# Three quarters of a 1024 x 4096 x 1024 float32 product by seven products of block sums in place of eight

## The chip, the core and the metric

One core of a Trainium2 chip runs the kernel. The metric is the device time of one execution in microseconds; for each kernel several executions are timed and the median is told. One further execution was recorded by the hardware profiler, and all rows below come from it. The engines are TensorE (PE; its weight loads are PEld), VectorE (DVE), ScalarE (ACT), GpSimd (POOL) and SyncE (SP), which issues most DMAs. POOL issues DMAs too. Each engine runs its own instructions in a fixed order, and a wait holds up everything behind it on that engine.

## The reference

One layer of a diffusion backbone on x of [1024, 1024], all in float32. The first sub-layer mixes tokens; the second, which the change is about, is an MLP with a squared ReLU:

```
def squared_relu_mlp(h, w1, w2):
    return jnp.square(jax.nn.relu(h @ w1)) @ w2
...
    h2 = modulate(x_lat, norm_pre_ffn[l], sh2, sc2)
    x_lat = x_lat + gt2 * rmsnorm(squared_relu_mlp(h2, w_ff1[l], w_ff2[l]), norm_post_ffn[l])
```

Here w1 is [1024, 4096] and w2 is [4096, 1024].

## The kernel before

Every large product is made of three matmuls: both factors are cut into a high and a low part of the type fp32r, and `mm3` (L196) sums high x high, high x low and low x high in PSUM. The cut is `split` (L165): ACT casts to the high part (L166), DVE subtracts it from the source for the low part (L167). `product` (L898) is one bank of PSUM, 128 x 512, with 4 steps of k, so 12 matmuls.

The program has three stages on PE after the attention: the output projection and the rows of x1 (`rows`, L946, with two calls of `rstd_of` for each tile of 128 rows), the first feed-forward product (loop over j, L1106), and the second (loop over blkn, L1163).

The first feed-forward product already works with seven products of block sums for each j of 0 to 15. A j is 256 of the 4096 hidden columns. Its four results c11, c12, c21 and c22 (two blocks of 128 hidden rows by two of 512 tokens) lie in one tile `hp`, of which there are two; ACT takes ReLU and square in place (L1152, L1153), and POOL writes the tile to `hid_d[j]` in HBM (L1154). The first two results of j = 0 to 3 were made earlier (`EARLY`). b_1 (in the buffer big0), b_2 (in big1), t1, t2 and t4 are the right-hand factors.

The second product is plain: eight blocks of 512 hidden rows; in each, two loads of hidden rows (`hr`, 1 MB each) are split into `hd` (big0 and big1 in turn), two loads of w2 (`wfraw`) are split into three pairs of buffers that take turns, and 8 token tiles x 2 column halves take 12 matmuls each, so 16 x 12 = 192 matmuls a block and 1,536 in all. ACT copies the results of block 0 to `y2t` (L1193), DVE adds those of the others (L1195). In the last block ACT sums squares (L1198), POOL multiplies by g2 (L1199), and DVE takes the reciprocal root (`rsqrt`, L206, for pairs of tiles and for the tiles 6 and 7 alone) and adds x1 (L1207); SP writes the output.

A scheduler writes the order of instructions on each engine down when the program is built, from its own estimate of times. The order is fixed from then on.

## Time and profile before

| | |
|---|---|
| median of 3 timed executions | 1721.79 us (1720.53 to 1725.85) |
| profiled execution | 1719.08 us |
| its span, first to last instruction | 1717.3 us |
| PE busy | 1650.3 us, 8,691 matmuls |
| DVE, ACT, POOL busy | 893.8, 612.0, 328.6 us |
| mean granted clock of PE | 0.988 of full speed |

The profiled execution lasted 1.8 us longer than its span, and was 2.7 us shorter than the median. Matmuls overlap, so that the busy time of one (0.39 us) is more than the distance between two starts.

### The profile page before, as it was taken

Reading aid. Unit: us, or ns where it says so; the run is one execution under the profiler, and the core shown is the slowest. Engines: PE = TensorE matmul, PEld = TensorE weight load, DVE = VectorE, ACT = ScalarE, POOL = GpSimd, SP = SyncE. Lnnn points to the kernel's source line nnn. Section 1 sums busy time; section 2 is a strip of 40 time slices with the busy share of each in tenths; the row PEclk is TensorE's granted clock in tenths of the full one; section 3 lists DMA queues with packets and bytes.
Section 4 is the critical chain, followed back from the end, with each engine's and each line's share of the span. In section 5 each row is a group of like instructions: output and inputs, shape, how many; then the busy total and the mean of one; then the engine's idle time right before and its main releaser. Section 6 shows DMA issues by size and latency. Waiting matters only on the chain. (4 is left out here: it accounts for less than half of the span.)

```text
span 1717.3 us, 22201 instructions
## 1 busy us (share of the span) xinstructions
PE 1650.3 (96%) x8691; PEld 1345.0 (78%) x8691; DVE 893.8 (52%) x1695; ACT 612.0 (36%) x882; POOL 328.6 (19%) x305
## 2 busy tenths in 40 slices
PE   5999999999999999989998997999999999999996
PEld 3889889988777777767786885788888888888885
DVE  4551253253445444476668669565556434444438
ACT  4321201112455555545255365443334521111111
POOL 1330021131322322468246000000000000000013
PEclk9999999999999999999999998999999999999998
DMA  9472544346423322385387224523322822222103
GB/s 323 159 178 85 165 145 157 118 146 201 124 90 116 109 68 74 105 233 161 116 286 241 108 83 142 164 95 128 115 98 98 306 99 98 99 98 74 50 25 147
DMA packets 150617, 233.05 MB, mean 136 GB/s; under 512 B 9248, under 2 KB 98344, under 8 KB 146928
## 3 DMA queue, kind: packets, MB, share of 16 engines
q1 hardware_dynamic: 143600, 202.57, 36.8%
q0 software_dynamic: 6912, 29.06, 4.8%
q8 instruction: 68, 1.11, 0.3%
q14 instruction: 37, 0.30, 0.1%
HBM read 173.70 MB, written 59.46 MB: 136 GB/s over the span
## 5 line engine op out<-in xcount | busy, mean ns | idle before, releaser
L166 ACT CAST wfhi<-wfraw 128x2048 fp32r<-128x2048 f32 (+2 forms) x59 | 84.9, 1469 | 377.5 <-PE sctx L202 216.5
L167 DVE TENSOR_TENSOR wflo<-wfraw,wfhi 128x2048 fp32r<-128x2048 f32 (+2 forms) x59 | 101.7, 1745 | 38.4 <-ACT wfhi L166 38.4
L200 PE MATMUL mm<-hT,wghi 128*128 128x512 f32 x256 | 103.0, 402 | 0.5 <-ACT stg L697 0.5
L201 PE MATMUL mm<-hT,wghi 128*128 128x512 f32 x256 | 101.0, 394 | 0.0
L202 PE MATMUL mm<-hT,wglo 128*128 128x512 f32 x256 | 100.7, 394 | 0.0
L1199 POOL TENSOR_TENSOR y2t<-y2t,g 128x512 f32<-128x512 f32 x16 | 20.4, 1291 | 331.9 <-issue 305.9
L167 POOL TENSOR_TENSOR wglo<-wgraw,wghi 128x1024 fp32r<-128x1024 f32 x20 | 48.2, 2408 | 134.5 <-ACT wghi L166 109.6
L167 DVE TENSOR_TENSOR winlo<-winraw,winhi 128x2048 fp32r<-128x2048 f32 (+1 forms) x16 | 30.5, 1925 | 75.5 <-ACT winhi L166 75.5
L1154 POOL DMA_DIRECT2D hid_d<-hp x16 | 8.6, 534 | 302.8 <-ACT hp L1153 254.6
L166 ACT CAST winhi<-winraw 128x2048 fp32r<-128x2048 f32 (+2 forms) x21 | 27.4, 1336 | 96.2 <-PE sctx L201 48.8
L200 PEld LDWEIGHTS mm<-hT,wghi 128*128 128x128 f32 x256 | 48.1, 188 | 10.8 <-issue 2.2
L202 PEld LDWEIGHTS mm<-hT,wglo 128*128 128x128 f32 x256 | 48.1, 188 | 9.2 <-issue 0.3
L201 PEld LDWEIGHTS mm<-hT,wghi 128*128 128x128 f32 x256 | 48.2, 188 | 7.6 <-issue 0.2
L202 PE MATMUL sloc<-hT,winlo 128*128 128x512 f32 x136 | 53.3, 392 | 0.0
L200 PE MATMUL sloc<-hT,winhi 128*128 128x512 f32 x136 | 53.2, 392 | 0.0
L201 PE MATMUL sloc<-hT,winhi 128*128 128x512 f32 x136 | 53.1, 390 | 0.0
L201 PE MATMUL sloc<-wflo,hd 128*128 128x512 f32 x128 | 50.3, 393 | 0.0
L201 PE MATMUL pt<-wflo,hd 128*128 128x512 f32 x128 | 50.3, 393 | 0.0
L201 PE MATMUL mm<-wflo,hd 128*128 128x512 f32 x128 | 50.3, 393 | 0.0
L200 PE MATMUL mm<-wfhi,hd 128*128 128x512 f32 x128 | 50.3, 393 | 0.0
L202 PE MATMUL sloc<-wfhi,hd 128*128 128x512 f32 x128 | 50.3, 393 | 0.0
L200 PE MATMUL sloc<-wfhi,hd 128*128 128x512 f32 x128 | 50.3, 393 | 0.0
(1132 smaller groups left out, 4979.3 us busy)
## 6 DMA issues: line engine op xcount, KB each, us to landing
wfraw<-in_w_ff_dram SPq DMA_DIRECT2D x32, 1024.0 KB
winraw<-in_w_ada_dram SPq DMA_DIRECT2D x24, 1024.0 KB
hr<-hid_d SPq DMA_DIRECT2D x16, 1024.0 KB
winraw<-in_w_in_dram SPq DMA_DIRECT2D x14, 1024.0 KB
hid_d<-hp POOLq DMA_DIRECT2D x12, 1024.0 KB, 6.2
wgraw<-in_w_in_dram SPq DMA_DIRECT2D x20, 512.0 KB
gates<-stg POOLq DMA_DIRECT2D x32, 256.0 KB, 3.7
gg<-gates SPq DMA_DIRECT2D x32, 256.0 KB
```

Source lines behind the costliest of these rows:

```text
L166: first = (hi_eng or a.copy)(hi_out, src)
L167: (lo_eng or v).tensor_tensor(lo_out, src, hi_out.bitcast(F32), op=ALU.subtract)
L200: pe.matmul(ps, lh, rh, start=(k == 0), stop=False)
L201: pe.matmul(ps, lh, rl, start=False, stop=False)
L202: pe.matmul(ps, ll, rh, start=False, stop=(k == ks - 1))
L1154: g.dma_start(hid_d[j][:, 512 * early:], hf)
L1199: g.tensor_tensor(y2t[:, t, hs], y2t[:, t, hs], g2[:, hs], op=ALU.mult)
```

## The change

In the second product, the hidden rows of j = 0 to 11 (three quarters, c4 = 0 to 2, of 1024 rows each) are treated as 2 x 2 blocks: two blocks f of hidden rows by two halves of tokens, times two by two blocks of w2. Seven products of block sums take the place of eight. Each of the seven has 4 token tiles of 12 matmuls, so 48, and a quarter has 336 in place of 384. Each of the seven kinds has one accumulator over the three quarters (m1 to m7, 128 x 4 x 512; m1 and m6 lie in big1). In quarter 0 ACT copies each result to its accumulator (L1260 of the changed kernel), in quarters 1 and 2 DVE adds it (L1262). In quarter 2 seven more additions of 128 x 2048 on DVE put the accumulators together into the four blocks of y2 (L1265 and one subtraction).

The left factors (`left`) are c11, c21 and c22 from `ha_d` and four sums from `hs_d`, each loaded with 1 MB and split into one of two slots `ops` in big0. The four sums (`hs`) are made in the first product: four DVE operations of 128 x 512 for each j below 12, with one more DMA to HBM. The right factors (`right`) need four DVE operations of 128 x 2048 for each quarter, done in place on the loaded w2 blocks. The last quarter (j = 12 to 15, blkn = 6 and 7) stays as it was. For j = 15 the order of the products becomes p7, p3, p6, p5. In the last two token tiles DVE multiplies by g2 in place of POOL, and `rsqrt` of one column needs two instructions for a step in place of three, with one more ahead.

```diff
@@ rsqrt
+        h = va
+        if n == 1:
+            h = p.tile([128, 1], F32, name="h", tag=tag + "_h", bufs=2)
+            v.tensor_scalar(h[:], va, -0.5, None, ALU.mult)
...
         for _ in range(3):
-            v.tensor_tensor(t[:], src, src, op=ALU.mult)
-            v.scalar_tensor_tensor(t[:], t[:], -0.5, va, ALU.mult, ALU.mult)
+            if n == 1:
+                v.scalar_tensor_tensor(t[:], src, h[:], src, ALU.mult, ALU.mult)
+            else:
...
@@ first product, loop over j
+        if j == 15:
+            p7, p3 = product(bank(), gb, 2, t3), product(bank(), gb, 1, b22)
...
-        g.dma_start(hid_d[j][:, 512 * early:], hf)
+        if j >= 12:
+            g.dma_start(hid_d[j - 12][:], hf)
+        else:
+            c4, q = divmod(j, 4)
+            if not early:
+                g.dma_start(ha_d[c4][:, 0, q], c11)
+            g.dma_start(ha_d[c4][:, 1:3, q], hp[:, 1])
+            hs = phr.tile([128, 4, 512], F32, name="hs", tag="hr")
+            v.tensor_tensor(hs[:, 0], c12, c22, op=ALU.add)
+            less(hs[:, 2], c11, c12)
+            less(hs[:, 1], c22, hs[:, 2])
+            less(hs[:, 3], c21, hs[:, 1])
+            g.dma_start(hs_d[c4][:, :, q], hs[:])
@@ second product
-        y2t = pf.tile([128, 8, D], F32, name="y2t")
+        m3, m5, m7, m4, m2 = (pf.tile([128, 4, 512], F32, name=f"m{k}") for k in (3, 5, 7, 4, 2))
+        both = big.tile([128, 4, 4, 512], F32, name="both", tag="big1")
+        m1, m6 = both[:, 0], both[:, 1]
+        ops = big.tile([128, 2, 2, 4, 512], F32R, name="ops", tag="big0")
...
+        def left(c4, i, first):
+            src = (ha_d[c4][:, 0], ha_d[c4][:, 1], hs_d[c4][:, 1], hs_d[c4][:, 3], hs_d[c4][:, 0], hs_d[c4][:, 2], ha_d[c4][:, 2])[i]
+            raw = m4[:] if first and i == 1 else php.tile([128, 4, 512], F32, name="hr", tag="hp", bufs=2)[:]
+            sy.dma_start(raw, src)
+            op = ops[:, next(count) % 2]
+            split(op[:, 0], op[:, 1], raw)
+            return op
+        def right(i, w):
+            w11, w21, w12, w22, _ = w
+            if i == 2:
+                less(w12, w22, w12)
+                v.tensor_tensor(w11, w11, w12, op=ALU.add)
+            if i == 4:
+                less(w22, w22, w11)
+                less(w11, w11, w21)
+            op = parts(next(wpool))
+            split(op[0][:], op[1][:], (w11, w21, w11, w22, w22, w12, w11)[i])
+            return op
...
+        for c4 in range(3):
+            w, new = home, None
+            for i, m in enumerate((m1, m2, m6, m3, m5, m7, m4)):
+                l, r = nxt
+                if i < 6:
+                    nxt = factors(c4, i + 1, w)
...
+                for t in range(4):
+                    p = psum(next(turn8))
+                    mm3(p[:], 4, lambda s_, k: l[:, s_, k, t * 128:(t + 1) * 128], lambda s_, k: r[s_][:, k, :])
+                    if c4 == 0:
+                        a.copy(m[:, t], p[:])
+                    else:
+                        v.tensor_tensor(m[:, t], m[:, t], p[:], op=ALU.add)
...
-        for blkn in range(8):
+        for blkn in range(6, 8):
...
-                        g.tensor_tensor(y2t[:, t, hs], y2t[:, t, hs], g2[:, hs], op=ALU.mult)
+                        (v if t >= 6 else g).tensor_tensor(y[cc], y[cc], g2[:, hs], op=ALU.mult)
```

The built order shows where the new work stands. On DVE, at the passage from the first product to the second (j = 15; `hp` is its result tile, `hd` and `ops` the low parts of left factors, `wflo` those of right factors), there stood before:

```order
L1132 TENSOR_TENSOR hp_11720<-hp_11720,pt_11751 128x512 [waits DMASW2_49,PE_49,Activation_49]
L167 TENSOR_TENSOR hd_11851<-hr_11852,hd_11851 128x2048 [waits Activation_49]
L167 TENSOR_TENSOR wflo_11869<-wfraw_11866,wfhi_11868 128x2048 [waits DMAHW6_49,PE_49,Activation_49]
L1132 TENSOR_TENSOR hp_11720<-hp_11720,mm_11765 128x512 [waits DVE_49,PE_49]
L1132 TENSOR_TENSOR hp_11720<-hp_11720,sloc_11779 128x512 [waits DVE_49,PE_49]
L1132 TENSOR_TENSOR hp_11720<-hp_11720,pt_11792 128x512 [waits DVE_49,PE_49]
L1132 TENSOR_TENSOR hp_11720<-hp_11720,pt_11792 128x512
L1132 TENSOR_TENSOR hp_11720<-hp_11720,po_11822 128x512 [waits DVE_49]
L1132 TENSOR_TENSOR hp_11720<-hp_11720,sctx_11805 128x512 [waits DVE_49,PE_49]
L167 TENSOR_TENSOR wflo_12108<-wfraw_12105,wfhi_12107 128x2048 [waits DMAHW7_49,Activation_49]
L167 TENSOR_TENSOR hd_12096<-hr_12097,hd_12096 128x2048 [waits DMAHW1_49,Activation_49]
L167 TENSOR_TENSOR hd_11851<-hr_11856,hd_11851 128x2048 [waits DMAHW2_49,Activation_49]
```

and now stand, with the two adds from `sctx` (the last product of j = 15) ahead of the first `ops`:

```order
L1145 TENSOR_TENSOR hp_11790<-hp_11790,pt_11821 128x512 [waits DMASW6_49,PE_49,Activation_49]
L1145 TENSOR_TENSOR hp_11790<-hp_11790,pt_11861 128x512 [waits DVE_49,PE_49]
L1145 TENSOR_TENSOR hp_11790<-hp_11790,mm_11835 128x512 [waits DVE_49]
L1145 TENSOR_TENSOR hp_11790<-hp_11790,sctx_11875 128x512 [waits DVE_49,PE_49]
L1145 TENSOR_TENSOR hp_11790<-hp_11790,sctx_11875 128x512
L1145 TENSOR_TENSOR hp_11790<-hp_11790,po_11892 128x512 [waits DVE_49]
L167 TENSOR_TENSOR ops_11933<-hr_11946,ops_11933 128x2048 [waits DMAHW4_49,Activation_49]
L1145 TENSOR_TENSOR hp_11790<-hp_11790,sloc_11848 128x512 [waits DVE_49]
L167 TENSOR_TENSOR wflo_11958<-both_11932,wfhi_11957 128x2048 [waits DMAHW5_49,Activation_49]
L908 TENSOR_TENSOR w2raw_11940<-both_11932,w2raw_11940 128x2048 [waits DMAHW6_49,DMAHW2_49]
L1225 TENSOR_TENSOR w2raw_11939<-w2raw_11939,w2raw_11940 128x2048 [waits DVE_49]
L167 TENSOR_TENSOR ops_11933<-m4_11927,ops_11933 128x2048 [waits DMAHW7_49,Activation_49]
```

So the low part of the first left factor stood behind one add of j = 15 and ahead of six (the seven rows L1132), and now stands behind six adds (the rows L1145) and ahead of one. It is followed by the low part of a right factor and two sums of w2 blocks.

In SP's queue at the same place (`hr` and `m4` are loads of left factors, `both` and `w2raw` of w2, `g2` a row) there stood before:

```order
L1175 DMA wfraw_12105<-in_w_ff2_dram 128x4x512 [waits DMAHW4_49,DVE_49]
L1162 DMA g2_11849<-grow1_161 128x1024 [waits PE_49]
L1169 DMA hr_12097<-hid_d2_8764 128x2048 [waits DMASW7_49,DMASW2_49,DVE_49]
L1169 DMA hr_11856<-hid_d1_8763 128x2048 [waits DMASW5_49,DMASW7_49,DMASW3_49,DMASW1_49]
L1175 DMA wfraw_12111<-in_w_ff2_dram 128x4x512 [waits DMAHW6_49,DVE_49]
```

and now:

```order
L1206 DMA w2raw_11940<-in_w_ff2_dram 128x4x512 [waits DMAHW0_49,DVE_49]
L1197 DMA g2_11937<-grow1_161 128x1024 [waits PE_49]
L1215 DMA hr_11946<-ha_d0_8766 128x2048 [waits DMASW5_49,DMASW2_49,DMASW7_49,DMASW0_49,Activation_49]
L1206 DMA both_11932<-in_w_ff2_dram 128x4x512 [waits PE_49]
L1206 DMA both_11932<-in_w_ff2_dram 128x4x512
L1215 DMA m4_11927<-ha_d0_8766 128x2048 [waits DMAHW7_49,PE_49]
L1215 DMA hr_12018<-hs_d0_8769 128x2048 [waits DMAHW4_49,DVE_49]
```

The first load of a left factor (`hr` from `ha_d0`) now waits for DMAs of POOL's queue (DMASW) and an ACT instruction, that is for the write of j = 14 to have left the `hp` tile that it takes over; two w2 loads, and then the second left factor, are queued behind it.

On DVE in the midst of the second product (before), the 16 adds of a block came with the low parts of two right and two left factors for the next block; of these three stand in this piece:

```order
L1195 TENSOR_TENSOR y2t_11845<-y2t_11845,po_13307 128x512 [waits DVE_49,PE_49]
L167 TENSOR_TENSOR hd_13566<-hr_13567,hd_13566 128x2048 [waits DMAHW2_49,Activation_49]
L1195 TENSOR_TENSOR y2t_11845<-y2t_11845,mm_13342 128x512 [waits DVE_49,PE_49]
L167 TENSOR_TENSOR hd_13566<-hr_13571,hd_13566 128x2048 [waits DMAHW7_49,Activation_49]
L1195 TENSOR_TENSOR y2t_11845<-y2t_11845,pt_13370 128x512 [waits DVE_49,PE_49]
L167 TENSOR_TENSOR wflo_13578<-wfraw_13575,wfhi_13577 128x2048 [waits DMAHW3_49,Activation_49]
L1195 TENSOR_TENSOR y2t_11845<-y2t_11845,sloc_13356 128x512 [waits DVE_49,PE_49]
L1195 TENSOR_TENSOR y2t_11845<-y2t_11845,mm_13384 128x512 [waits DVE_49,PE_49]
L1195 TENSOR_TENSOR y2t_11845<-y2t_11845,sloc_13398 128x512 [waits DVE_49,PE_49]
```

and now, in quarter 2 (products m2 and m6), stand:

```order
L167 TENSOR_TENSOR ops_11933<-hr_12929,ops_11933 128x2048 [waits DMAHW5_49,Activation_49]
L1262 TENSOR_TENSOR m2_11931<-m2_11931,sloc_12939 128x512 [waits PE_49]
L167 TENSOR_TENSOR wflo_13001<-both_11932,wfhi_13000 128x2048 [waits Activation_49]
L1262 TENSOR_TENSOR m2_11931<-m2_11931,pt_12953 128x512 [waits PE_49]
L908 TENSOR_TENSOR both_11932<-both_11932,w2raw_11939 128x2048 [waits DVE_49]
L1262 TENSOR_TENSOR m2_11931<-m2_11931,sctx_12967 128x512 [waits PE_49]
L908 TENSOR_TENSOR w2raw_11939<-w2raw_11939,both_11932 128x2048 [waits DVE_49]
L1262 TENSOR_TENSOR m2_11931<-m2_11931,po_12981 128x512 [waits PE_49]
L167 TENSOR_TENSOR ops_11933<-hr_12996,ops_11933 128x2048 [waits DMAHW6_49,Activation_49]
L1262 TENSOR_TENSOR both_11932<-both_11932,mm_13004 128x512 [waits PE_49]
L1265 TENSOR_TENSOR m2_11931<-m2_11931,both_11932 128x2048 [waits DVE_49]
L167 TENSOR_TENSOR wflo_13069<-both_11932,wfhi_13068 128x2048 [waits Activation_49]
```

Each product of four adds now comes with the low parts of one left and one right factor for a later product, and with sums of w2 blocks (L908) or of accumulators (L1265) besides.

## Rows read from the trace of the kernel before

**Rows 1.** The page: busy time, share of the span and instructions of each engine.

```profile
PE 1650.3 (96%) x8691; PEld 1345.0 (78%) x8691; DVE 893.8 (52%) x1695; ACT 612.0 (36%) x882; POOL 328.6 (19%) x305
```

**Rows 2.** Stretches: busy time of each engine, granted clock, DMA share, GB/s.

```profile
1042.00:1066.00 24.00, 13.52 (x48) 9.97 (x48) 24.00 (x24) 10.25 (x11) 0.54 (x1) 0.89 0.53 149
...
1106.00:1346.00 240.00, 239.10 (x1038) 194.24 (x1038) 143.10 (x174) 95.56 (x75) 6.41 (x12) 1.00 0.33 117
...
1391.00:1436.00 45.00, 45.00 (x196) 36.54 (x196) 20.15 (x20) 8.58 (x6) 0.00 (x0) 1.00 0.26 94
```

**Rows 3.** Waits of TensorE from 1060 us to the end, complete: total, times, longest.

```profile
PE sloc L200 <- ACT t L166: 5.4, 1, 5.4
PE sloc L200 <- ACT wfhi L166: 0.9, 1, 0.9
PE pt L200 <- ACT wfhi L166: 0.6, 1, 0.6
```

**Rows 4.** Timeline of TensorE: first and last of the last stage's 1,536 matmuls.

```profile
1346.46 0.40 PE L200 MATMUL mm<-wfhi,hd 128*128 128x512 f32 x1
...
1701.80 0.39 PE L202 MATMUL po<-wfhi,hd 128*128 128x512 f32 x1
```

**Rows 5.** Groups of instructions from 1106 us on, by line and form.

```profile
L167 DVE TENSOR_TENSOR wflo<-wfraw,wfhi 128x2048 fp32r<-128x2048 f32 x28 | 63.9, 2288 | 35.2 <-ACT wfhi L166 35.2
...
L1195 DVE TENSOR_TENSOR y2t<-y2t,mm 128x512 f32<-128x512 f32 x28 | 19.2, 686 | 33.0 <-PE mm L202 33.0
...
L166 ACT CAST wfhi<-wfraw 128x2048 fp32r<-128x2048 f32 x28 | 53.3, 1906 | 243.7 <-PE sctx L202 216.5 <-PE po L201 13.4 <-PE sctx L201 7.3
...
L1193 ACT COPY y2t<-mm 128x512 f32<-128x512 f32 x4 | 2.4, 589 | 2.9 <-PE mm L202 2.9
```

**Rows 6.** Timeline around the last stage's start: ScalarE, GpSimd, VectorE, SyncE's queue.

```profile
1332.33 1.91 ACT L1153 ACTIVATE hp<-hp 128x2048 f32<-128x2048 f32 x1
...
1334.53 0.53 POOL L1154 DMA_DIRECT2D hid_d<-hp  x1 [19.44 <-ACT hp L1153]
...
1346.66 0.69 DVE L1132 TENSOR_TENSOR hp<-hp,sctx 128x512 f32<-128x512 f32 x1 [0.43 <-PE sctx L202]
...
1356.10 0.34 SPq L1169 DMA_DIRECT2D hr<-hid_d  x1
...
1365.13 1.91 ACT L166 CAST hd<-hr 128x2048 fp32r<-128x2048 f32 x1 [9.57 <-DMA hr<-hid_d]
```

**Rows 7.** DMA issues, us to landing: the page, then 1340 to 1660 us alone.

```profile
hid_d<-hp POOLq DMA_DIRECT2D x12, 1024.0 KB, 6.2
...
hid_d<-hp POOLq DMA_DIRECT2D x1, 1024.0 KB, 9.1
```

**Rows 8.** Stretches: granted clock, DMA share and GB/s (TensorE's busy time ahead).

```profile
1045.00:1047.00 2.00, 1.84 (x8) 1.00 0.70 182
...
1066.00:1071.00 5.00, 4.42 (x11) 0.50 0.21 76
...
1334.00:1340.00 6.00, 1.00 1.06 415
```

**Rows 9.** Timeline of TensorE: two of its waits at the third stage's start.

```profile
1045.15 0.50 PE L202 MATMUL mm<-b,wflo 128*128 128x512 f32 x1 [2.27 <-DVE wflo L167]
...
1065.60 1.22 PE L200 MATMUL sloc<-t,wfhi 128*128 128x512 f32 x2 [5.45 <-ACT t L166]
```

**Rows 10.** Timeline of VectorE and GpSimd in the last 20 us.

```profile
1697.75 1.13 DVE L216 SCALAR_TENSOR_TENSOR t<-t,va 128x2 f32<-128x2 f32 x1
...
1703.47 2.49 POOL L1199 TENSOR_TENSOR y2t<-y2t,g 128x512 f32<-128x512 f32 x2 [4.60 <-ACT jk L1198]
...
1704.78 1.19 DVE L216 SCALAR_TENSOR_TENSOR t<-t,va 128x1 f32<-128x1 f32 x1
...
1706.67 0.16 DVE L215 TENSOR_TENSOR t<-r 128x1 f32<-128x1 f32 x1
...
1707.49 1.24 DVE L215 TENSOR_TENSOR t<-r 128x1 f32<-128x1 f32 x1
```

More of the change, by code (lines that the diff above doesn't have):

```diff
@@ L889, in block_kernel @@
     K2, EARLY = 4, 4
-    hid_d, c12_d = scratch("hid_d", 16, [128, 2 * N]), scratch("c12_d", EARLY, [128, 512])
+    c12_d = scratch("c12_d", EARLY, [128, 512])
+    ha_d, hs_d = (scratch(o, 3, [128, k, 4, 512]) for o, k in (("ha_d", 3), ("hs_d", 4)))
+    hid_d = scratch("hid_d", 4, [128, 2 * N])
     wfa = pool(ctx, "wfa", 1, side="right", tags=("hi", "lo"))
@@ L1112, in block_kernel @@
             sy.dma_start(c12, c12_d[j][:])
+            sy.dma_start(c11, ha_d[0][:, 0, j])
         if early:
@@ L1141, in block_kernel @@
         add(c12, c12, p6)
-        if j > 0:
+        if j == 15:
+            p5 = product(bank(), gb, 3, t1)
+        elif j > 0:
             p7, p5, p3 = product(bank(), gb, 2, t3), product(bank(), gb, 3, t1), product(bank(), gb, 1, b22)
@@ L1159, in block_kernel @@
         pf = pool(s, "pf", 1, side="right")
-        y2t = pf.tile([128, 8, D], F32, name="y2t")
+        m3, m5, m7, m4, m2 = (pf.tile([128, 4, 512], F32, name=f"m{k}") for k in (3, 5, 7, 4, 2))
+        both = big.tile([128, 4, 4, 512], F32, name="both", tag="big1")
+        m1, m6 = both[:, 0], both[:, 1]
+        ops = big.tile([128, 2, 2, 4, 512], F32R, name="ops", tag="big0")
         g2 = pf.tile([128, D], F32, name="g2")
         sy.dma_start(g2[:], bcast_rows(grow[1][0], D))
-        for blkn in range(8):
+        home = [*(rawp.tile([128, 4, 512], F32, name="w2raw", tag="raw", bufs=2)[:] for _ in range(2)), both[:, 2], both[:, 3],
+                phr.tile([128, 4, 512], F32, name="w2raw", tag="hr")[:]]
@@ new lines, in block_kernel, with w2_load @@
+        home = [home[k] for k in (0, 2, 1, 3, 4)]
+        def w2_load(c4, b, out_):
+            cc, f = divmod(b, 2)
+            sy.dma_start(out_, w_ff2[0, c4 * 1024:(c4 + 1) * 1024, cc * 512:(cc + 1) * 512].rearrange(
+                "(q f p) n -> f p q n", f=2, p=128)[f])
+        count = itertools.count()
+        def left(c4, i, first):
[5 more added lines that the diff above has]
+            return op
@@ new lines, in right, with factors @@
+        def right(i, w):
[9 more added lines that the diff above has]
+            return op
+        def factors(c4, i, w):
+            return left(c4, i, c4 == 0), right(i, w)
@@ new lines, in block_kernel, with plus @@
+        for b in range(4):
+            w2_load(0, b, home[b])
+        nxt = factors(0, 0, home)
+        for c4 in range(3):
[4 more added lines that the diff above has]
+                    nxt = factors(c4, i + 1, w)
+                    if c4 < 2:
+                        if i == 0:
+                            home = [w[4], w[1], w[3], w[2], w[0]]
+                            w2_load(c4 + 1, 0, home[0])
+                        if i == 3:
+                            w2_load(c4 + 1, 1, home[1])
+                            w2_load(c4 + 1, 2, home[2])
+                        if i == 4:
+                            w2_load(c4 + 1, 3, home[3])
+                elif c4 < 2:
+                    nxt = factors(c4 + 1, 0, home)
+                for t in range(4):
[5 more added lines that the diff above has]
+                        v.tensor_tensor(m[:, t], m[:, t], p[:], op=ALU.add)
+                if c4 == 2:
+                    def plus(x, y):
+                        v.tensor_tensor(x[:], x[:], y[:], op=ALU.add)
+                    if i == 1:
+                        plus(m2, m1)
+                    if i == 2:
+                        plus(m6, m1)
+                        plus(m7, m6)
+                    if i == 4:
+                        plus(m6, m5)
+                        plus(m3, m6)
+                    if i == 5:
+                        plus(m5, m7)
+                    if i == 6:
+                        less(m4[:], m7[:], m4[:])
@@ L1180, in block_kernel @@
             for t in range(8):
+                y = [y2[t // 4][cc][:, t % 4] for cc in range(2)]
                 if blkn == 7:
@@ L1203, in block_kernel @@
                     r = rstd_of(pf, ss[:, 0, :n], n, f"o{n}")
-                    for i, (t_, x1) in enumerate(group):
+                    for i, (t_, y_, x1) in enumerate(group):
                         for cc in range(2):
                             hs = slice(cc * 512, (cc + 1) * 512)
-                            v.scalar_tensor_tensor(x1[:, hs], y2t[:, t_, hs], r[:, i:i + 1], x1[:, hs], ALU.mult, ALU.add)
+                            v.scalar_tensor_tensor(x1[:, hs], y_[cc], r[:, i:i + 1], x1[:, hs], ALU.mult, ALU.add)
                             sy.dma_start(out[0, t_ * 128:(t_ + 1) * 128, hs], x1[:, hs])
```

21 lines of the change are left out of this document (10 added, 11 removed).

## The prediction

> **What bounds the kernel now.** I read the page's busy shares first: TensorE is busy 96% of the span, no other engine over 52% [rows 1]. A share mixes stages, so next the stretches around the edits. In the first feed-forward product TensorE works 239.10 of 240 us while VectorE works 143.10 and ScalarE 95.56; in the midst of a block of the second product it works 45.00 of 45 us, at a granted clock of 1.00, beside 20.15 us of VectorE and 94 GB/s of DMA. Only the stretch 1042 to 1066 us is another engine's: VectorE works 24.00 of 24 us and TensorE 13.52 [rows 2]. TensorE's waits, last, say whether anything is left to gain by feeding it better: from 1060 us to the end there are three, the last two under a microsecond [rows 3]. So after 1066 us time is bought by matmuls left out, and lost by any wait that comes new. The pitch of the last stage is (1701.80 − 1346.46) / 1535 = 0.2315 us between two starts [rows 4]; twelve matmuls take 2.78 us, a product of 48 takes 11.1 us.
>
> **Matmuls left out.** Three quarters lose one product of eight each: 3 × 48 = 144 matmuls, 144 × 0.2315 = 33.3 us. This is the change's whole income on TensorE, and it holds as long as TensorE stays without waits.
>
> **The last token tiles.** After the last matmul VectorE's small operations of the reciprocal root take 0.16 us alone, but three of them took 1.13, 1.24 and 1.19 us where GpSimd was multiplying [rows 10]. With the last four multiplications on VectorE these waits go: 3.56 − 3 × 0.16 = 3.1 us. VectorE pays four operations of 128 x 512, 4 × 0.686 = 2.7 us [rows 5], though not all of it stands on the path; GpSimd's 2.49 us for two [rows 10] leave it. The root of one column is a net two instructions shorter (three saved, one added), and tiles 6 and 7 each take one: 2 × 2 × 0.16 = 0.6 us. Sum −1.0 us; the bounds are 0 (all four multiplications on the path, one slow operation kept) and −2.5 us (half of them beside ScalarE's squares). The same root in the rows of x1 runs in the stage where TensorE has no gap, or in the stretch that VectorE's large operations fill; two operations of 0.16 us a tile move nothing there that I can price: 0, at most 2 us either way.
>
> **The first product.** Each j below 12 gets four more VectorE operations of 128 x 512 with both sources in SBUF. Taken at 0.69 us each (the same shape as [rows 5]), this is 2.7 us a j. Twelve j's fill the 240 us of [rows 2], 20 us each, of which VectorE has some 12 filled; 14.7 of 20 still leave room, the sums follow ScalarE's square of the same tile, and the next operands are made earlier. TensorE's cover here is the eight banks and operands one product ahead: I cost this at 0. If the cover were gone it would cost up to 2.7 us a j. GpSimd issues three DMAs a j in place of one, 0.53 us each [rows 6]; 1 MB more a j takes the traffic from 117 to about 170 GB/s, beside a stretch that reached 415 [rows 8].
>
> **The passage to the second product (the added wait).** Before, the first left factor was in place long before TensorE came to it. Now it can be loaded only into the `hp` tile of j = 14, after that tile has gone to HBM. All up to here stands where it stood, so I use the old clock. ScalarE's square of j = 14 ends at 1334.24, GpSimd issues the write at 1334.53 [rows 6]. It lands 6.2 us later by the median, 9.1 us by this one [rows 7]: 1340.7 to 1343.6, middle 1342.2. The load is 1 MB: 2.5 us at the 415 GB/s of [rows 8], or 9.0 us as from issue to cast in [rows 6] (1356.10 to 1365.13). I take 5, between: the queue is quieter than there, but two w2 loads stand right behind. So 1347.2; the cast of 1.91 us gives 1349.1. VectorE meanwhile ends the six adds that stand ahead. The add that takes the last product of j = 15 began at 1346.66 [rows 6]; now three of them, 0.69 us each, start from there (two from `sctx`, one from `po`), so VectorE is free at 1348.7. The cast is later, and the subtraction, 2.29 us [rows 5], ends at 1351.4. TensorE can start with the high parts, 4 steps of high x high and high x low in two tiles at most, if it is let; the order of `mm3` asks for a low part at the third matmul. I give it 8 matmuls, 1.85 us, of useful work: an effective start at 1349.55 in place of 1346.46, **a wait of 3.1 us**. The floor is 2.7 us (data there in time, VectorE's order alone), the ceiling 8.5 (9.1 us for the write and 9.0 for the load). What the clock does after such a wait is a term of its own: a wait of 2.27 us left the granted clock at 1.00, one of 5.45 us [rows 9] was followed by 5 us at 0.50, that is at 1.2 GHz, with 11 matmuls [rows 8] where 5 us at the pitch hold 21.6, a loss of 2.5 us. The wait here is nearer to the first: I take 1.1. **Sum +4.2 us**, from +2.7 (0 if TensorE finds more high parts to do than I grant it) to +11.
>
> Behind the first subtraction on VectorE stand a right factor's low part, two sums of w2 and the second left factor. At 2.29 us each, and one add, these end at 1361.3; product 2 is due 11.1 us after 1349.55, at 1360.7, and the clock's term makes that 1361.8: level, inside the bounds above. From product 3 on each factor has a product's time.
>
> The Trainium skill, "DMA: Bandwidth & Descriptors", section "Bandwidth", puts a transfer of 1 MB alone at 6.15 us, 341 GB/s, against the 415 GB/s that several transfers at once show here [rows 8]. By the page the load would come about 1.2 us later than the 5 us I took, and the sum would be 1.2 us higher; by the row alone it would be 2.5 us earlier, and VectorE's order would be the limit.
>
> **The second product.** A product of 11.1 us needs on VectorE two subtractions and four adds: 2 × 2.29 + 4 × 0.686 = 7.3 us [rows 5]. A quarter adds four sums of w2 blocks, 9.2 us. Quarter 1: 7 × 7.3 + 9.2 = 60.4 of 7 × 11.1 = 77.8 us. Quarter 0 has no adds on VectorE: ScalarE has 14 casts of 1.91 and 28 copies of 0.589 [rows 5], 43 of 77.8 us. Quarter 2 has seven sums of accumulators besides, 16.0 us: 76.4 of 77.8 us. The two products with two of them or with w2 sums besides need 11.9 against 11.1; the factors stand a product ahead and eight banks hold two products of adds, so an excess of 0.8 us is carried. I cost it at 0, with up to 6 us if each wait for a sum's input falls into VectorE's way. The loads are 1 MB of left factor a product and 4 MB of w2 a quarter, 1.57 MB (1.65e6 bytes) in 11.1 us, about 150 GB/s against 94 [rows 2].
>
> **The sum.** −33.3 − 1.0 + 4.2 = −30.1 us. The profiled execution took 1719.08 us (span 1717.3 and 1.8 around it), so 1689.0; the median of the runs shown lies 2.7 us above it, so **1691.7 us**.
>
> **The rivals.** (A) As summed: 1688 to 1698. (B) The passage costs nothing: the load is quicker than I take it and TensorE works on high parts meanwhile; 4.2 us less, 1687.5. For it: the stretch of 415 GB/s [rows 8]; against it: six adds stand ahead of the subtraction, whatever the load does. (C) The passage at its long end (+11) and VectorE late in quarter 2 (+5): about 1703. For it: 9.1 us for that very write [rows 7] and 9.57 us of ScalarE's wait for such a load [rows 6]; against: these were measured with four loads in the queue. (D) Slower: VectorE becomes the bound of quarters 1 and 2, because each subtraction must wait for its cast on ScalarE. In [rows 5] VectorE's 28 subtractions of right factors have 35.2 us of waiting for the cast ahead of them. If both casts of a product (2 × 1.91) stood in VectorE's way, it would take (60.4 / 7 + 3.8) = 12.4 us a product in quarter 1 and 14.7 in quarter 2: (1.3 + 3.6) × 7 = 34 us, which eats the gain, and stalls of this kind at each product would bring stretches at 1.2 GHz as in [rows 8]: some 15 us more, 1741. It decides from 13.3 us a product over the fourteen on (30.1 / 14 above 11.1). Against it: the factors are asked for a product ahead, and ScalarE has 3.8 us of casts in 11.1. (E) The change doesn't do what it says, the matmuls go and waits of the same length come: the same place as D with half its price, 1716 to 1722.
>
> **Chances.** A 0.60, B 0.15, C 0.17, D 0.04, E 0.04. About 0.3%, 5 us, is what a measurement of this kernel can tell from no change. A, B and C are all faster by more: 0.92, with a part of E 0.93; same 0.03, slower 0.04. Eight in ten: A with B and the nearer part of C, 1685 to 1703; the low end is B with the bound of the tail (−1.5) and 1 us of the small roots.
>
> **What would show it.** TensorE should have 8,691 − 144 = 8,547 matmuls, and from the first of product 1 to the last 1392 × 0.2315 = 322 us. One wait of TensorE of about 3 us should stand before product 1's third matmul, released by VectorE's `ops` (L167), and perhaps a stretch at 0.50 behind it; none of over a microsecond after. VectorE's busy time should go to about 1,000 us: sums of hidden rows +33, 18 more subtractions +41, w2 sums +27, accumulators +16, 24 adds fewer −16, multiplications +3. ScalarE's goes up by some 40 us; quarter 2 has VectorE full. From the last matmul to the end it should be some 14 us. I am wrong if the wait at the passage is over 6 us, if VectorE's factors in quarter 2 release TensorE, or if the first product shows waits where it had none.

## The result and the profile after

The changed kernel takes 1698.51 us (median of 4, 1694.81 to 1707.3) where the kernel before takes 1723.82 (median of 4): ratio 0.9857, 95% interval 0.9809 to 0.9905. The profiled execution has a span of 1695.9 us, 21.4 less than before. So it is faster, by 25 us of the 30 that were summed up.

The busy times of the page, the line that answers to [rows 1]:

```profile
PE 1622.1 (96%) x8547; PEld 1321.3 (78%) x8547; DVE 982.2 (58%) x1724; ACT 651.6 (38%) x912; POOL 338.9 (20%) x321
```

There are 144 matmuls fewer, as there should be. TensorE's waits from 1030 us to the end, which answer to [rows 3] (total, times, longest; [rows 3] begin at 1060 us, and from 1030 us on the kernel before had two more of over a microsecond, 2.5 and 2.3):

```profile
PE pt L200 <- ACT wfhi L166: 8.0, 2, 6.3
PE mm L200 <- ACT ops L166: 3.3, 1, 3.3
PE pt L993 <- ACT xn L982: 2.3, 1, 2.3
PE mm L200 <- ACT wfhi L166: 1.3, 1, 1.3
PE mm L202 <- DVE wflo L167: 1.2, 1, 1.2
...
PE sctx L200 <- ACT wfhi L166: 1.1, 1, 1.1
PE sloc L200 <- ACT wfhi L166: 0.9, 1, 0.9
PE sloc L202 <- DVE wflo L167: 0.8, 1, 0.8
...
PE mm L202 <- DVE ops L167: 0.2, 1, 0.2
```

The one long wait on a left factor (`ops`) was foreseen. Of the others, one is for the last rows of x1 (`xn`), and most are for w1 (`wfhi`, `wflo`) at the start of the first product and in it. To see what they cost, I compared the two traces matmul by matmul: up to the second product both kernels run 7,155 matmuls, so the start of the nth can be set against the start of the nth before. The table (worked out from the timelines of TensorE) says how much further each kernel fell behind the kernel before in each stretch, then how long the second product took from its first matmul to its last, and the time from there to the end. Before, these last two were 355.3 and 15.5 us. Each delay is the median over the matmuls of a stretch: those that the kernel before starts at 880 to 900, 1000 to 1030, 1075 to 1110 and 1150 to 1340 us, and then the first matmul of the second product. The rows from swap_casts on are the experiments of the next section. The kernel before was profiled once; root_only, which is that kernel but for the root, agrees with it to 0.03 us in the last two of these stretches.

```
us behind the kernel before  to 900us  rows x1  j=0 start  j=4 passage  to 2nd product  2nd   tail
changed                         1.1     -0.1      +3.8        +6.7           +3.4       322.1  12.4
changed_again                   5.9      0.0      +3.3        +4.6           +3.1       323.2  12.4
swap_casts                      5.5     +1.9      +3.8        +5.2           +3.6       323.0  12.4
sums_on_pool                    0.8     +1.5      +4.2        +4.8           +3.5       323.3  12.4
no_early_sums                   7.9     +1.3      +4.1        +0.1           +3.2       322.2  12.4
no_early_sums_no_c11            4.6     -0.4      +3.7        +0.5           +3.7       323.3  12.6
old_root_rows                   5.1     +2.1      +0.2        +4.6           +3.9       323.1  12.5
root_only                       9.6     -0.2      +3.7         0.0            0.0       355.4  14.4
left_in_spare                   1.3     -0.3      +3.6        +4.6           -0.1       329.7  12.4
left_in_spare_2                 5.0     +0.4      +3.5        +4.6           -0.1       322.5  12.4
multiply_on_pool                7.4     +1.6      +4.0       +10.5           +3.6       323.3  14.1
combined                        8.4     -0.1      +0.2        +4.3           -0.1       322.7  12.5
combined_2                      0.3     +1.6      +0.7        -0.4            0.0       322.7  12.5
```

The first row adds up: 14.9 us behind at the second product (1361.38 against 1346.46 in [rows 4]), 33.2 us won in it, 3.1 in the tail, together the 21.4 us of the span. Some 10.5 us were lost at two places that I had costed at nothing. The first column covers instructions that stand in the same order on every engine in all fourteen profiles, and yet it differs by up to 9 us from execution to execution; so a span alone can't tell effects of 3 us apart, but the stretches can. (Some expectations below give 5.8 us for the passage to j = 4: that is the step from 5.6 to 11.5 us, counted from some us later than the 6.7 of the table.)

The passage to the second product in the changed kernel, from the timelines of GpSimd, SyncE's queue, ScalarE, VectorE and TensorE, answering to [rows 6]:

```profile
1346.02 0.53 POOL L1173 DMA_DIRECT2D hid_d<-hp  x1 [19.44 <-ACT hp L1171]
...
1352.35 0.34 SPq L1215 DMA_DIRECT2D hr<-ha_d  x1
...
1359.42 1.90 ACT L166 CAST ops<-hr 128x2048 fp32r<-128x2048 f32 x1 [13.70 <-DMA hr<-ha_d]
...
1361.36 2.29 DVE L167 TENSOR_TENSOR ops<-hr,ops 128x2048 fp32r<-128x2048 f32 x1 [1.37 <-ACT ops L166]
...
1361.38 0.50 PE L200 MATMUL mm<-wfhi,ops 128*128 128x512 f32 x1 [3.31 <-ACT ops L166]
1363.70 0.50 PE L202 MATMUL mm<-wfhi,ops 128*128 128x512 f32 x1 [0.21 <-DVE ops L167]
```

The chain is the one forecast: write of j = 14, load, cast, subtraction. The write is over at the latest when the load is issued, 6.3 us after its own issue; the load took 7.1 us to the cast. TensorE starts on high parts as soon as the cast ends and is nearly done with them when the low part comes, 2.3 us later. The granted clock stayed at 1.00 behind this wait (stretches 1360 to 1368 us; columns as in [rows 2]), the first two lines; in the second profile of the same kernel, changed_again, a wait of 3.02 us was followed by a stretch at 0.50, the third line:

```profile
1360.00:1364.00 4.00, 2.41 (x9) 1.72 (x10) 2.65 (x2) 2.98 (x2) 0.00 (x0) 1.00 1.06 416
1364.00:1368.00 4.00, 4.00 (x19) 3.27 (x18) 3.96 (x3) 3.87 (x4) 0.00 (x0) 1.00 0.96 370
...
1364.00:1366.00 2.00, 2.00 (x6) 1.61 (x5) 2.00 (x2) 1.46 (x1) 0.00 (x0) 0.50 1.07 427
```

Eight profiles have this wait (3.0 to 3.8 us). In six of them some 3.5 us at 0.50 came behind it, and their second products took 323.0 to 323.3 us; in two (changed and no_early_sums) the clock stayed at 1.00, and they took 322.1 and 322.2. So the clock's price here was 0 or about 1 us from one execution to the next.

The second product has no other wait, and VectorE has room in each quarter (it was busy 50.5 of 78 us in quarter 0; quarters 1 and 2 are shown):

```profile
1439.00:1517.00 78.00, 78.00 (x338) 63.08 (x338) 57.04 (x45) 26.48 (x15) 0.00 (x0) 1.00 0.39 135
1517.00:1595.00 78.00, 78.00 (x338) 63.05 (x338) 67.86 (x51) 27.85 (x15) 0.00 (x0) 1.00 0.45 154
```

### The profile page after: what moved, and what is told of

Same layout as the page of the kernel before. It is cut to its first block, busy times and chain, and to the rows that moved or that the text cites. A ratio compares the mean times of both kernels' runs of the same rounds, so it can differ in the third digit from the quotient of the medians.

```text
span 1695.9 us, 21997 instructions
## 1 busy us (share of the span) xinstructions
PE 1622.1 (96%) x8547; PEld 1321.3 (78%) x8547; DVE 982.2 (58%) x1724; ACT 651.6 (38%) x912; POOL 338.9 (20%) x321
## 5 line engine op out<-in xcount | busy, mean ns | idle before, releaser
L166 ACT CAST wfhi<-wfraw 128x2048 fp32r<-128x2048 f32 (+2 forms) x47 | 62.0, 1357 | 175.7 <-PE sloc L201 36.9
L166 ACT CAST ops<-hr 128x2048 fp32r<-128x2048 f32 x20 | 38.2, 1909 | 113.2 <-PE mm L201 42.7
L167 DVE TENSOR_TENSOR wflo<-wfraw,wfhi 128x2048 fp32r<-128x2048 f32 (+2 forms) x47 | 74.2, 1605 | 5.8 <-ACT wfhi L166 5.8
L167 DVE TENSOR_TENSOR winlo<-winraw,winhi 128x2048 fp32r<-128x2048 f32 (+1 forms) x16 | 30.8, 1948 | 76.4 <-ACT winhi L166 76.4
L167 POOL TENSOR_TENSOR wglo<-wgraw,wghi 128x1024 fp32r<-128x1024 f32 x20 | 48.2, 2408 | 134.6 <-ACT wghi L166 134.5
L1312 POOL TENSOR_TENSOR m<-m,g 128x512 f32<-128x512 f32 x12 | 15.3, 1294 | 292.6 <-ACT jk L1311 292.6
L167 DVE TENSOR_TENSOR ops<-hr,ops 128x2048 fp32r<-128x2048 f32 x20 | 45.8, 2290 | 32.0 <-ACT ops L166 32.0
L166 ACT CAST winhi<-winraw 128x2048 fp32r<-128x2048 f32 (+2 forms) x21 | 27.4, 1335 | 95.5 <-PE sctx L201 48.8
L201 PE MATMUL mm<-hT,winhi 128*128 128x512 f32 x120 | 47.4, 395 | 0.0
L415 DVE SCALAR_TENSOR_TENSOR ev<-winraw,cs,ev 128x512 f32<-128x512 f32 x56 | 44.6, 797 | 3.9 <-DMA winraw<-in_w_ada_dram 2.2
L202 PE MATMUL mm<-hT,winlo 128*128 128x512 f32 x120 | 46.8, 390 | 0.0
L607 POOL TENSOR_TENSOR tb<-tt,mask 128x128 f32<-128x128 f32 x56 | 29.4, 553 | 86.4 <-DVE mc L655 47.0
L200 PE MATMUL mm<-hT,winhi 128*128 128x512 f32 x120 | 46.4, 393 | 0.0
```

The source lines that it names most:

```text
L166: first = (hi_eng or a.copy)(hi_out, src)
L167: (lo_eng or v).tensor_tensor(lo_out, src, hi_out.bitcast(F32), op=ALU.subtract)
L200: pe.matmul(ps, lh, rh, start=(k == 0), stop=False)
L201: pe.matmul(ps, lh, rl, start=False, stop=False)
L202: pe.matmul(ps, ll, rh, start=False, stop=(k == ks - 1))
L415: v.scalar_tensor_tensor(ev[:], w[:, k, :], s_, ev[:], ALU.mult, ALU.add)
```

## The experiments

### Where the first product loses time

At the passage from j = 3 to j = 4 the old kernel's VectorE was full, although it worked only 143 of the 240 us from 1106 us on [rows 2]; two stretches of the kernel before (columns as in [rows 2], VectorE's third):

```profile
1112.00:1116.00 4.00, 3.10 (x12) 1.93 (x12) 3.88 (x6) 3.00 (x4) 0.00 (x0) 1.00 0.00 0
1116.00:1120.00 4.00, 4.00 (x19) 3.29 (x18) 3.93 (x7) 2.04 (x2) 0.53 (x1) 1.00 0.31 127
```

In the changed kernel the same place reads so (timelines of VectorE, ScalarE and TensorE; L1180 is a sum of hidden rows, L924 the last of four sums of a w1 block, L166 and L167 its cast and subtraction):

```profile
1112.92 0.69 DVE L1180 TENSOR_TENSOR hs<-hp 128x512 f32<-128x512 f32 x1 [2.48 <-DMA hs_d<-hs]
...
1128.42 0.68 DVE L924 TENSOR_TENSOR wfraw<-wfraw 128x512 f32<-128x512 f32 x1
...
1128.29 3.70 ACT L166 CAST wfhi<-wfraw 128x2048 fp32r<-128x2048 f32 x2 [3.78 <-PE pt L201]
...
1130.24 0.50 PE L200 MATMUL pt<-t,wfhi 128*128 128x512 f32 x1 [1.75 <-ACT wfhi L166]
1132.04 0.79 PE L200 MATMUL sctx<-t,wfhi 128*128 128x512 f32 x1 [1.07 <-ACT wfhi L166]
```

Three things could make the cast late: VectorE reaches L924 late; ScalarE casts j = 5 ahead of j = 4, and that cast waits for TensorE; or a result tile is held too long. From 1130.8 us, about when the second wait began, to 1137.7 the granted clock was at 0.50; two stretches of 2 us out of it:

```profile
1132.00:1134.00 2.00, 1.96 (x5) 1.58 (x6) 2.00 (x2) 0.00 (x0) 0.00 (x0) 0.50 1.04 387
1134.00:1136.00 2.00, 2.00 (x6) 1.56 (x5) 0.71 (x1) 0.00 (x0) 0.00 (x0) 0.50 0.95 241
```

Five or six matmuls stand there in 2 us, where 2 / 0.2315 is 8.6. In changed_again the same two waits of 1.75 and 1.07 us came at this place and the clock stayed at 1.00; 4.6 us were lost there in place of 6.7. So 2 us or more of the 6.7 are the clock's, and they don't come in each execution.

**swap_casts** turns the two casts alone:

```diff
...
-            sums(raw)
-            gb = part_sums(raw, next(wpool))
+            with behind(chain[-1] if j == 5 else None):
+                sums(raw)
+                gb = part_sums(raw, next(wpool))
+            if j == 4:
+                chain.append(last_cast[0])
```

> The changed kernel with one order turned back: ScalarE casts the block sums of w1 for j = 4 ahead of those for j = 5 (in the changed kernel j = 5 stood first, and its cast waits for TensorE); nothing else moves. In the changed kernel TensorE falls behind the old kernel by 5.8 us there (from 5.6 to 11.5 us). Theory 1 (VectorE is late: the sums of hidden rows of j = 2 and 3 and two waits for transfers stand ahead of the w1 sums): the sums for j = 4 end at 1129.1 us whatever stands first, so at most 1 to 2 us come back, profiled span 1694 to 1695. Rival (the swapped casts are the cause): the whole 5.8 us come back, span near 1690.

Measured: 1702.66 us, ratio 0.9848 (0.9822 to 0.9873), and 5.2 us lost at the passage. The swapped casts are not the cause.

**sums_on_pool**:

```diff
-            v.tensor_tensor(hs[:, 0], c12, c22, op=ALU.add)
...
+            e = g if early else v
+            e.tensor_tensor(hs[:, 0], c12, c22, op=ALU.add)
...
```

> The changed kernel with the four sums of hidden rows for j = 0 to 3 made by GpSimd in place of VectorE. Theory 1 (VectorE's load at the passage from j = 3 to j = 4): the fall of 5.8 us behind the old kernel there goes, span near 1690; the casts come back into the old order too, so the rival of the swapped casts expects the same here, and the two are told apart by the other run. Rival: GpSimd is slower at a sum (1.3 us or more each against 0.69) and holds the result tile longer, whose next load then comes late, so that VectorE waits for that load: no gain, or up to 5 us slower.

Measured: 1703.4 us, ratio 0.986 (0.9836 to 0.9885), 4.8 us lost. The rival's forecast came: no gain. VectorE waits for the reload of the result tile, as it says, but TensorE's one long wait there is for a subtraction that GpSimd's sums slowed (timelines of VectorE, GpSimd and, last, TensorE):

```profile
1103.34 0.69 DVE L1145 TENSOR_TENSOR hp<-hp,pt 128x512 f32<-128x512 f32 x1 [9.25 <-DMA hp<-c_d]
...
1115.81 0.69 DVE L1145 TENSOR_TENSOR hp<-hp,po 128x512 f32<-128x512 f32 x1 [8.41 <-DMA hp<-c_d]
...
1121.42 0.68 DVE L1145 TENSOR_TENSOR hp<-hp,pt 128x512 f32<-128x512 f32 x1
...
1123.22 3.98 DVE L167 TENSOR_TENSOR wflo<-wfraw,wfhi 128x1024 fp32r<-128x1024 f32 x2
...
1124.50 2.15 POOL L1184 TENSOR_TENSOR hs<-hp,hs 128x512 f32<-128x512 f32 x1
...
1125.56 0.50 PE L202 MATMUL sloc<-b,wflo 128*128 128x512 f32 x1 [2.61 <-DVE wflo L167]
```

The pair of subtractions at 1123.22 (a 128 x 1024 and a smaller one) took 3.98 us beside GpSimd's sums; the add from PSUM at 1121.42 took no longer than elsewhere. How the late start and the slowing share the loss was not told apart. In the changed kernel the same pair reads:

```profile
1120.06 1.82 DVE L167 TENSOR_TENSOR wflo<-wfraw,wfhi 128x1024 fp32r<-128x1024 f32 x2
```

**no_early_sums** and **no_early_sums_no_c11** leave the sums of j = 0 to 3 out, the second also the load of c11 (the edit of the first):

```diff
+            if early:
+                g.dma_start(hs_d[c4][:, :, q], hp[:].rearrange('p f t n -> p (f t) n'))
+                continue
             hs = phr.tile([128, 4, 512], F32, name="hs", tag="hr")
```

> The changed kernel without the four sums of hidden rows for j = 0 to 3: the result tile itself is written in their place, so the bytes stay and the sums of quarter 0 are left out of the computation. Between the passage to j = 0 and the steady part the changed kernel falls 4.6 to 6.7 us behind the old one in five runs, also with the sums on GpSimd and with the casts swapped back. Theory 2 (result tiles: a tile is only loaded anew after its sums and writes, the sums wait for the one buffer of the sums before to be written, and VectorE, which waits for the reload, runs late): without the sums the fall is under 2 us. Rival (the new load of c11 alone holds VectorE): 4 us or more stay.

> As no_early_sums, and without the load of c11 for j = 0 to 3 (two of the result tile's four blocks are written twice in place of the sums; quarter 0 of the second product is then not the reference's). Both theories: the fall at the passage to j = 4 is under 1 us, as in the old kernel. If it stays at 4 us or more, neither the sums nor the load of c11 is the cause, and the transfers (POOL's two more issues a j, 1 MB more written) are what is left.

Measured: 0.1 and 0.5 us lost at the passage (single executions of 1699.52 and 1696.23 us, whose other stretches are in the table). So the sums are the whole cause, and the load of c11 none; and as ScalarE's order is that of the changed kernel in both runs, the swapped casts are cleared once more. But the reason given in theory 2 fell with the same trace, for VectorE waits for the reloaded tile longer than ever and nothing is lost:

```profile
1115.07 0.69 DVE L1145 TENSOR_TENSOR hp<-hp,pt 128x512 f32<-128x512 f32 x1 [14.15 <-DMA hp<-c_d]
```

What counts is what VectorE has to do behind such a wait and ahead of the w1 sums. combined and combined_2, below, test it.

### The start of the first product

**old_root_rows** and **root_only** put the new root in the last tiles alone, and in the kernel before alone (the edit of old_root_rows):

```diff
-        if n == 1:
+        if n == 1 and tag[0] == 'o':
```

> The changed kernel with the old reciprocal root in the rows of x1 (the short one stays in the last tiles). In the changed kernel TensorE is 1.0 us late against the old one before j = 0 and 4.5 us after it. Theory: the shorter root alone moved the order on VectorE there (sums that wait for a w1 load now stand ahead of the sums of transposed rows), so 3.5 us come back, span near 1692.4. Rival: the order there moved for other reasons (the new load of c11, the later sums), and nothing comes back: 1695 to 1697.

> The kernel before with the shorter root of one column alone, nothing else of the change. Theory (the root alone moves VectorE's order at the start of the first product): TensorE falls 3.5 us further behind there, and the tail is at most 0.6 us shorter: 2 to 4 us slower than before. Rival (the fall needs the new load of c11 and the sums too): no fall at j = 0, 0 to 1 us faster.

Measured: with the old root 0.2 us lost at j = 0 (median 1699.76 us, ratio 0.9838, 0.9818 to 0.9859), with the new root alone 3.7 us (one execution, 1731.05 us; 9.6 us of its delay come from the part before 900 us). The span of old_root_rows (1697.9 us, where 1692.4 was expected) hides the gain, as 5.1 us were lost ahead of it, before 900 us. So the root alone makes the loss at j = 0. Its instructions are shorter; it is the order that differs, and it differs from the first rows on. The larger part is lost at the last rows. In all ten profiles with the new root in the rows TensorE's transposes wait 2.29 us for ScalarE's normalized rows (`xn`), and in none of the four with the old root. In the changed kernel VectorE's steps of that root are split by an add (L1082) that itself waits for TensorE (the last line is the kernel before, where the same `xn` followed its root):

```profile
1028.97 0.16 DVE L225 SCALAR_TENSOR_TENSOR r<-t,it 128x1 f32<-128x1 f32 x1
1030.41 0.69 DVE L1082 TENSOR_TENSOR st<-st,mm 128x512 f32<-128x512 f32 x1 [1.28 <-PE mm L202]
...
1032.33 1.13 ACT L982 ACTIVATE xn<-x,r 128x1024 f32<-128x1024 f32 x1
...
1033.52 0.55 PE L993 MATMUL pt<-ident,xn 128*128 128x128 f32 x3 [2.29 <-ACT xn L982]
```

```profile
1027.61 1.15 ACT L970 ACTIVATE xn<-x,r 128x1024 f32<-128x1024 f32 x1 [0.64 <-DVE r L217]
```

Behind that, VectorE waits for a w1 load ahead of the sums of transposed rows (`q<-th`), which begin 5.2 us later than before. The two lines of the changed kernel, then the one of before:

```profile
1039.78 0.69 DVE L921 TENSOR_TENSOR wfraw<-wfraw 128x512 f32<-128x512 f32 x1 [3.43 <-DMA wfraw<-in_w_ff_dram]
...
1044.05 1.22 DVE L908 TENSOR_TENSOR q<-th 128x1024 f32<-128x1024 f32 x1
```

```profile
1038.81 1.22 DVE L896 TENSOR_TENSOR q<-th 128x1024 f32<-128x1024 f32 x1
```

### The passage to the second product

**left_in_spare**:

```diff
-            raw = m4[:] if first and i == 1 else php.tile(
+            raw = m4[:] if first and i == 1 else home[4] if first and i == 0 else php.tile(
```

> The changed kernel with the first left factor loaded into the spare w2 tile, which is free long before, in place of the hp tile of j = 14. Theory: the wait of 3.3 us ahead of the second product goes (it is the chain write of j = 14, load, cast, subtraction), span near 1692.6. Rival: VectorE's order is the limit, as six adds stood ahead of the subtraction, or the next factors become late, since a w2 load and the second factor now come later: a wait of 2 us or more stays at the first or second product.

Measured: 1705.86 us, ratio 0.9866 (0.9838 to 0.9894). The passage lost nothing, but the second product took 7.6 us longer, for one wait (timelines of TensorE, ScalarE and SyncE's queue):

```profile
1353.57 0.34 SPq L1215 DMA_DIRECT2D m<-ha_d  x1
...
1370.62 1.90 ACT L166 CAST ops<-m 128x2048 fp32r<-128x2048 f32 x1
...
1372.57 0.80 PE L200 MATMUL sloc<-wfhi,ops 128*128 128x512 f32 x1 [5.84 <-ACT ops L166]
```

The second left factor's load stood last in the queue, and its cast behind three others on ScalarE, one of which, the third factor's, itself waited 1.22 us for TensorE. Both sides were half right: the first wait went, and what stood behind it made a new one. Some 7 us at a granted clock of 0.50 came with this wait, so that 5.8 us of waiting cost 7.6.

**left_in_spare_2** gives the second factor the tile that comes free first:

```diff
+            raw = home0[4] if first and i == 0 else m4[:] if first and i == 2 else php.tile(
...
+                        if i == 2:
                             w2_load(c4 + 1, 0, home[0])
```

> As left_in_spare (first left factor in the spare w2 tile), with the second left factor in the hp tile of j = 14 and the third in m4, and the next quarter's first w2 load asked for two products later. In left_in_spare the wait of 3.4 us ahead of product 1 went, but product 2 waited 5.84 us for its left factor, whose load stood last of six. Theory (loads queue up here, and the order of them decides): neither product waits over 1 us, and the passage is 3.4 us shorter than in the changed kernel, second product 322 to 323 us long. Rival (too many bytes for the time, whatever their order): 2 us or more stay at product 2.

Measured: 1698.81 us, ratio 0.986 (0.983 to 0.989); no wait on a left factor is left, −0.1 us at the passage and 322.5 us for the second product. So it was the order of loads and casts, and not the bytes.

### The tail

**multiply_on_pool**:

```diff
-                        (v if t >= 6 else g).tensor_tensor(y[cc], y[cc], g2[:, hs], op=ALU.mult)
+                        g.tensor_tensor(y[cc], y[cc], g2[:, hs], op=ALU.mult)
```

> The changed kernel with the last two tiles' products with g2 on GpSimd again. From the last matmul to the end it was 15.5 us before and is 12.4 now. Theory (GpSimd's multiplication holds VectorE's small operations up, and these products are on the path): about 2.5 us come back, 14.5 to 15.2. Rival (the shorter root made the gain): 12.4 to 13.

Measured: a tail of 14.1 us, and in root_only, which has the new root but GpSimd's products, 14.4. So of the 3.1 us the root gives 1.1 to 1.4 and the products on VectorE 1.7 to 2.0: both sides hold a part. Small operations of one column that GpSimd holds up are back behind the last matmul (1696.71), which the changed kernel has none of there; the operations on pairs of tiles ahead of it are slow in both kernels (1.19 and 1.22 us in the changed one). Timelines of VectorE and GpSimd:

```profile
1700.92 0.22 DVE L221 SCALAR_TENSOR_TENSOR t<-r,h 128x1 f32<-128x1 f32 x1
1701.15 1.26 POOL L1312 TENSOR_TENSOR m<-m,g 128x512 f32<-128x512 f32 x1 [0.28 <-ACT jk L1311]
1701.17 1.25 DVE L225 SCALAR_TENSOR_TENSOR r<-t,r 128x1 f32<-128x1 f32 x1
```

Its median (1708.67 us, ratio 0.9886, 0.9845 to 0.9927) tells little of the tail: the profiled execution lost 10.5 us at j = 4, where the same order lost 4.6 and 6.7 in the two profiles of the changed kernel. Of what differs the clock is one part, at 0.50 for 10.4 us there against none and 6.9; why VectorE's waits were longer stays open.

### All turned back at once

**combined** joins left_in_spare_2, the old root in the rows and a rule for the sums of j = 3 (`late` makes them), with swap_casts:

```diff
+            if j == 4:
+                cast4 = last_cast[0]
+                with behind(cast4):
+                    late()
```

> Three turns of the changed kernel at once: left_in_spare_2, the old root in the rows of x1, and the four sums of hidden rows for j = 3 put behind ScalarE's cast of the w1 sums of j = 4, with the casts of j = 4 and 5 in the old order. From the profiles so far: 3.4 us come back at the passage to the second product and 3.4 us at j = 0; at j = 4, 4.6 to 6.7 us were lost and none without the early sums. Theory 1 (VectorE's queue at that passage): with one of the two sets of sums behind the w1 sums at least 2.5 us of it come back, 9 to 11 us in all, 1687 to 1690 where the changed kernel has 1698. Rival (the early sums hold the result tile, wherever they stand): nothing comes back at j = 4, 6.8 us in all, 1691 to 1693.

Measured: 1694.65 us, ratio 0.9804 (0.9782 to 0.9827). Two losses went, the one at j = 4 stayed at 4.3 us, as the rival says (the time is above both ranges, beside 8.4 us lost before 900 us in the profile). But the trace shows that the sums had not moved: the rule names an instruction of ScalarE, and by this trace it moved nothing in VectorE's queue. VectorE's sum of hidden rows (L1188) still stands ahead of L924, and the cast waits for L924:

```profile
1126.45 0.69 DVE L1188 TENSOR_TENSOR hs<-hp 128x512 f32<-128x512 f32 x1
...
1131.27 0.69 DVE L924 TENSOR_TENSOR wfraw<-wfraw 128x512 f32<-128x512 f32 x1
...
1131.99 3.70 ACT L166 CAST wfhi<-wfraw 128x2048 fp32r<-128x2048 f32 x2 [4.64 <-DVE wfraw L924]
```

**combined_2** names VectorE's own instruction, the last w1 sum of j = 4, for the sums of j = 3 and, by the same rule, for the w1 sums of j = 5:

```diff
-                with behind(cast4):
+                with behind(sum4):
                     late()
```

> As combined, with the order on VectorE now really turned. In combined the sums of j = 3 still stood between the w1 sums (the rule given only moved ScalarE's queue), and 4.3 us were lost at the passage to j = 4. Now the four w1 sums of j = 4 stand in one row, and the four sums of hidden rows of j = 3 and the w1 sums of j = 5 stand behind them. Theory 1 (VectorE's queue): the cast that TensorE waits for starts 4 to 5 us earlier, and 3 us or more of the 4.3 come back, 1690 to 1692 where combined had 1694.65 with the kernel before at 1726.26. Rival (sums hold the result tile wherever they stand): 4 us stay.

> The changed kernel once more, on the same chip as combined_2, to compare the two and to see how far its own profiles differ. All theories: 1695 to 1703, with 3.5 to 4 us lost at j = 0, 4.6 to 6.7 at j = 4 and 3.4 at the passage to the second product.

Measured: 1688.41 us (1685.66 to 1691.22), somewhat under the 1690 to 1692 expected, ratio to the kernel before 0.9786 (0.9761 to 0.9811); the changed kernel on the same chip 1702.0 (1700.35 to 1703.6), 0.9863 (0.9839 to 0.9886). So 13.6 us come back with the same matmuls, by the old root, by other tiles and by order; the stretches from j = 0 on account for 11 of them. This version beats both kernels. At j = 4 nothing is lost. The four w1 sums stand in one row, and the cast follows at once, 4.8 us after the first matmul of j = 4 (1116.70); in combined it came 9.4 us after it (1122.56):

```profile
1120.73 0.69 DVE L924 TENSOR_TENSOR wfraw<-wfraw 128x512 f32<-128x512 f32 x1
...
1121.46 1.91 ACT L166 CAST wfhi<-wfraw 128x2048 fp32r<-128x2048 f32 x1 [0.18 <-DVE wfraw L924]
```

VectorE still does the same sums there, a few places later. Theory 1 holds, in the form: not VectorE's load, but sums that nobody waits for soon, ahead of four that TensorE waits for. Two sets moved, the four sums of hidden rows of j = 3 and the four w1 sums of j = 5; in no_early_sums the two sets of w1 sums still alternate on VectorE and nothing is lost, so it is the sums of hidden rows that count.

## Why the prediction was right or wrong

The sign, the range (1685 to 1703) and the likeliest mechanism hold. The time of 1698.5 lies just past case A's own range, and not for the reason that case C gave. That the range holds is luck in part: its upper end was meant for a longer passage and a late VectorE in quarter 2, and 10.5 us that the sum has at nothing took that room. By steps:

- **Matmuls left out**: right, 355.3 − 322.1 = 33.2 us for 33.3.
- **The last token tiles**: right in mechanism, mis-sized: −3.1 us, past the bound of −2.5, for −1.0. The products on VectorE brought 1.7 to 2.0 us for 0.4 (3.1 less 2.7), and the root 1.1 to 1.4 for 0.6. One reading was wrong: the slow operation of 1.13 us at 1697.75 stands ahead of the last matmul (1701.80), and not after it.
- **The root in the rows**: wrong. "Two operations of 0.16 us a tile move nothing there that I can price: 0, at most 2 us either way". They moved the built order, and that cost 3.3 to 4.2 us, 2.29 of it in TensorE's wait for the last rows, shown by old_root_rows and root_only.
- **The first product**: with the root in the rows, this is the step that failed. "14.7 of 20 still leave room ... I cost this at 0". The mean over 240 us hid the one place where VectorE was full before (3.88 and 3.93 of 4 us), and the sums of j = 0 to 3 fall ahead of it. It cost 6.7 us in the first profile, 4.6 to 5.2 in five others and 10.5 in one; in the first profile the two losses together are 10.5 us.
- **The passage**: right: a wait of 3.3 us and 3.4 lost for 3.1. The parts were less right than their sum: the write was over by 6.3 us after its issue for 7.7, the load took 7.1 for 5, and the two errors nearly cancel. The wait was for ScalarE's cast, where VectorE's subtraction was named; the high parts hid what the subtraction took, as assumed, but for 0.2 us. The clock's term of 1.1 was nothing in the first profile (1.00 after the wait) and about 1 us in six of the eight profiles with this wait.
- **The second product**: right at 0. VectorE was busy 67.9 us in quarter 2 where 76.4 were counted; 51 of its 53 instructions lie in that stretch, and neighbours overlap a little.
- **The rivals**: D (VectorE the bound of the second product) and E were not seen. That the first product would show waits where it had none was named as what would make the forecast wrong, and that is what came.

## What to carry to other kernels

Where an in-order engine has room on average, look for the stretches of a few us in which it has none before calling new work hidden, above all where one loop form goes over into another. Here the same sums cost 4.6 us or more ahead of work that TensorE waits for, and nothing behind it; and a rule of order helped only when it named an instruction of the queue where the two stand. A small edit far from the gain can move the built order too, so the order is worth comparing wherever the edit reaches. A changed wait should be followed to the loads and casts behind it: left_in_spare removed one wait of 3.3 us and got one of 5.8.

## What the runs showed of the hardware

- GpSimd's sums slowed VectorE's subtractions of two SBUF sources from 1.82 to 3.98 us a pair, while VectorE's adds from PSUM beside them stayed at 0.68. The Trainium skill, "GPSIMD Engine Reference", section "Specifications", says that GpSimd's SBUF interface is shared with VectorE and contends with VectorE's instructions that have two SBUF inputs; the rows of sums_on_pool agree.
- The same instructions in the same order, before 900 us, took up to 9 us more in some executions than in others; the granted clock of the whole span lay at 0.982 to 0.991. The cause stays open.
- What TensorE's clock did behind a wait differed between executions of one program. In the changed kernel's two profiles waits of 1.75 and 1.07 us came with 6.9 us at 0.50 (1.2 GHz) in one and with none in the other, and waits of 3.31 and 3.02 us before the second product with none in the first and 3.5 us in the other. A wait of 5.84 us (left_in_spare) came with 6.9 us at 0.50 and cost 7.6 us in all.
